# A hybrid mLSTM, GLA and sparse-attention block: one weight place more, one load in flight fewer, one large tile fewer, and a planner that counts changes of matmul kind

## The chip, the cores and the metric

The kernel runs on one core of a Trainium2 chip. A core has TensorE (PE, matrix multiply, with weight loads listed apart as PEld), VectorE (DVE), ScalarE (ACT), GpSimd (POOL) and SyncE (SP, which here only issues transfers), each with its own instruction stream; they meet at semaphores. The metric is device time of one execution in microseconds (us).

## The reference, cut to what matters

```python
def hybrid_layer(x, ...):                       # x: 1 x 512 x 1024, f32
    p = split_columns(rmsnorm(x, norm_g) @ w_in)
...
    hm = mlstm_chunkwise(q, k, v, li, lf)       # 4 heads of 256, behind a causal convolution and silu
    y_ml = rmsnorm(hm * sigmoid(ml_o)) * silu(ml_z)
    hg = gla_chunked(gla_q, gla_k, gla_v, la)   # 4 heads, chunks of 64
    y_gla = rmsnorm(hg) * silu(gla_r)
    hd = dsa_sparse_attention(dq, dk, dsa_v, iq, idx_k, iw, rel_bias, topk=128)
    y_dsa = hd * silu(dsa_z)
    return x + concatenate([y_ml, y_gla, y_dsa]) @ w_out

def reference(x, ...):
    for layer in range(2):
        x = hybrid_layer(x, ...)
    return x
```

## The kernel before, in words

Most of PE's work is the two projections of each layer. They are done to about f32 precision with one-pass f32r matmuls: weights and activations are split into a high and a low part, and three matmuls (`mm3`: high x high, low x high, high x low) make one product. The names: `xs` is the normed block of x before its transpose, `psx` the transpose, `xhi` and `xlo` its two parts; `pn`, `pt` and `pw` are the outputs of projections in PSUM (128x512). Between them lie matmuls of another kind (transposes, f32 matmuls): `psx`, `psga` (the decayed products of GLA; its operands `dec` and `qz` are made by POOL, ACT and DVE), `psq` (transposes of `qn`, the normed queries and keys of the sparse attention), and others. `psS` are the one-pass products of `ml_q` and `ml_k`. `zz` and `so` are gates, `sw` the mLSTM decay weights, for which the mask `negm` is loaded; `bs` is the bias of the sparse attention, loaded from `skew` and masked by POOL with `sel`, the result of the top-k selection (pairs of MAX8 and MATCH_REPLACE on DVE); `rq` is the scale of `qn`.

Weights come in 178 pieces of 128x1024 f32 (512 KB). SP loads a piece into `raw`; ACT copies it to `hi` in f32r; DVE makes `lo` = `raw` - `hi`. All three come from one pool of `W_BUFS` places of that size. `make_room` issues loads as long as places are free and fewer than `RAWS` pieces are loading or unsplit; it runs after each `lo` and after each `give_back`, which frees the two places of a piece after its last matmul. A piece counts as loaded `LOAD` = 4.5 us after its issue. The pool `t4` has `N_T4` large tiles of 4 KB per partition for everything else that is large.

The order of all instructions is decided while the program is built. Each instruction is recorded through a `Meter`, which asks `cost` for a duration and books it on a `Clock` per engine, with the dependencies. Work beside the projections (softmax, selection, gates, GLA, mLSTM) is written as generators in a `Background`; each `tick` between groups of 6 projection matmuls first calls `prepare` (at most one `lo` and one `hi`) and then steps those tasks that are due by the clock of PE. So any change of a cost or a pool shifts where tasks are put between the projection matmuls, on every engine. On the chip each engine takes its instructions in this order and waits at semaphores.

All instructions are recorded at one line, L178, so the rows below are told apart by their tiles.

```python
    def prepare():
        if half_done:
            p = half_done.pop()
            lo = w_tile("lo", F32R)
            nc.vector.tensor_sub(lo, p.raw, p.hi.bitcast(F32))
...
            make_room()
        if to_split and to_split[0].loaded <= clock.at["pe"] and state["used"] + 2 <= W_BUFS:
            p = to_split.pop(0)
...
            p.hi = w_tile("hi", F32R)
            nc.scalar.activation(p.hi, p.raw, AF.Copy)
            half_done.append(p)
```

Of the kernel before, what the change touches and what calls it, by code (L numbers as in the profile page):

```python
# [159 lines left out]
def free_size(ap):  # L160
    return math.prod(ap.shape[1:])


class Meter:


    def __init__(self, engine, name, clock):
        self.engine, self.name, self.clock = engine, name, clock
# [12 lines left out]
    def cost(self, op, args, kw):  # L181
        out = args[0]
        if op == "dma_start":
            return None
        if self.name == "pe":
            if op == "transpose":
                return 0.109
            n, one_pass = free_size(out), kw["rhs"].dtype == F32R
            if one_pass:
                return max(n, 256) / 2210 + 0.002  # L190
            if out.shape[0] == 64:
                return max(n / 950, 0.08)
            return max(4 * n, 256) / 2400 + 0.004
        n = free_size(args[1]) if op == "max" else free_size(out)
        pointers = sum(hasattr(v, "ap") and free_size(v) == 1 for v in (*args[2:], *kw.values()))
        accum = kw.get("accum_out") is not None
        if self.name == "act":
            switch = self.clock.ln != (args[2] == AF.Ln)
            self.clock.ln = args[2] == AF.Ln
            return 0.155 + n / 1138 + 0.09 * pointers + 0.12 * accum + 1.3 * switch  # L200
        if self.name == "dve":
            return 0.15 + n / 945 + 0.06 * min(pointers, 1) + 0.02 * accum
        if kw.get("op") == OP.pow:
            return 0.45 + 0.15 * n
        return 0.1 + n / (510 if op == "tensor_tensor" else 600) + 0.1 * (op == "tensor_tensor")


class Clock:
# [4 lines left out]
    def __init__(self):  # L213
        self.at = dict(pe=0.0, act=0.0, dve=0.0, pool=0.0, sync=0.0)
        self.now = 0.0
        self.ln = True
        self.written, self.touched = {}, {}
        self.rings = {}

    def begin(self):  # L220
        self.now = self.at["pe"]
# [29 lines left out]
    def book(self, engine, cost, outs, ins):  # L251
        at = self.at
        start = max([at[engine]] + [self.latest(self.written, engine, v) for v in ins]
                    + [self.latest(self.touched, engine, v) for v in outs])
        if cost is None:
            at[engine] = start + self.ISSUE
            end, engine = start + self.DMA, "dma"
        else:
            at[engine] = end = start + cost
        self.now = max(self.now, end)  # L260
        for v in outs:
            self.written.setdefault(v.name, {})[self.box(v)] = end, engine
        for v in outs + ins:
            self.touched.setdefault(v.name, {})[self.box(v)] = end, engine
# [69 lines left out]
def hybrid_kernel(ctx, tc, a, out, dbg=None):  # L334
# [12 lines left out]
            nc.gpsimd.dma_start(dbg[name], ap)  # L347

    ctx.enter_context(tc.manual_schedule())
    N_T4, N_T2 = 11, 19  # L350
    W_BUFS, RAWS, LOAD = 11, 3, 4.5
    const = ctx.enter_context(tc.tile_pool(name="const", bufs=1))
    par = ctx.enter_context(tc.tile_pool(name="par", bufs=2))
    wp = ctx.enter_context(tc.tile_pool(name="wp", bufs=2))
# [997 lines left out]
```

## Time and profile before

| what | value |
|---|---|
| runs, median of 3 | 1228.73 us (1228.69 to 1230.84) |
| profiled execution | 1227.63 us |
| its span, first to last instruction | 1225.9 us |
| mean granted clock of PE | 0.996 |
| busy: PE, PEld | 1198.3 us (98%), 970.6 us (79%) |
| busy: DVE, ACT, POOL | 835.1 us (68%), 600.6 us (49%), 171.0 us (14%) |
| transfers | 107.70 MB, 88 GB/s on the mean |

The profiled execution is 1.1 us faster than the median; 1.7 us of it lie outside the span. Busy shares are means over stages: PE's 98% says that it nearly always has a matmul under way, not that each runs at its fastest. In a timeline row, the numbers are the start, the duration of the row (of all instructions that it groups), the engine, the operation with its output and inputs, and in brackets the idle time ahead of it and what released it.

### The profile page before, as it was taken

How to read it: one execution, taken by the hardware profiler on the slowest of the kernel's cores; microseconds unless marked ns; L12 is line 12 of the kernel's file. 1: busy time of each engine (PE TensorE's matmuls, PEld its weight loads, DVE VectorE, ACT ScalarE, POOL GpSimd, SP SyncE). 2: the span in 40 equal slices, each digit the busy share in tenths (PEclk: the TensorE clock that was granted, in tenths of full speed). 3: DMA queues.
4: the chain of work that ended last, by engine and by line, in shares of the span. 5: the costliest groups of instructions: out<-in, count | busy, mean ns of one | idle time of the engine just before them, and what ended most of it. 6: DMA issues, size and time to landing. Idle time of an engine off the chain costs nothing. (4 is left out here: it accounts for less than half of the span.)

```text
span 1225.9 us, 16513 instructions
## 1 busy us (share of the span) xinstructions
PE 1198.3 (98%) x6004; PEld 970.6 (79%) x6004; DVE 835.1 (68%) x1650; ACT 600.6 (49%) x1334; POOL 171.0 (14%) x309
## 2 busy tenths in 40 slices
PE   6999899999999999999999999999999999999998
PEld 4877687888888887788879777888788888778887
DVE  5477797876777765355555888879867867544644
ACT  6565446554344354652366654474443443555421
POOL 2001221321000010210010023031210000122000
PEclk8999999999999999999999999999999999999999
DMA  5333122212332234132124222222222223233221
GB/s 195 108 98 104 44 92 72 86 61 55 105 108 69 70 119 129 53 112 86 69 70 128 63 86 79 80 73 86 71 70 86 79 85 104 70 112 112 69 82 73
DMA packets 35152, 107.70 MB, mean 88 GB/s; under 512 B 5028, under 2 KB 8388, under 8 KB 35072
## 3 DMA queue, kind: packets, MB, share of 16 engines
q1 hardware_dynamic: 33136, 104.89, 26.5%
q0 software_dynamic: 1200, 1.36, 0.3%
q8 instruction: 47, 0.77, 0.3%
q10 hardware_dynamic: 736, 0.41, 0.1%
q14 instruction: 33, 0.27, 0.1%
HBM read 104.48 MB, written 3.43 MB: 88 GB/s over the span
## 5 line engine op out<-in xcount | busy, mean ns | idle before, releaser
L178 DVE TENSOR_TENSOR lo<-raw,hi 128x1024 fp32r<-128x1024 f32 x178 | 219.1, 1231 | 140.2 <-ACT hi L178 133.5
L178 PE MATMUL pn<-hi,xhi 128*128 128x512 f32 x768 | 313.4, 408 | 0.4 <-ACT xhi L178 0.4
L178 PE MATMUL pn<-lo,xhi 128*128 128x512 f32 x768 | 305.2, 397 | 4.1 <-DVE lo L178 4.1
L178 PE MATMUL pn<-hi,xlo 128*128 128x512 f32 x768 | 304.1, 396 | 0.0
L178 ACT ACTIVATE hi<-raw 128x1024 fp32r<-128x1024 f32 x178 | 188.7, 1060 | 197.9 <-PE pn L178 96.8
L178 PEld LDWEIGHTS pn<-lo,xhi 128*128 128x128 f32 x768 | 145.1, 189 | 37.7 <-DVE lo L178 7.0
L178 PEld LDWEIGHTS pn<-hi,xlo 128*128 128x128 f32 x768 | 144.6, 188 | 35.8 <-DVE xlo L178 1.3
L178 PEld LDWEIGHTS pn<-hi,xhi 128*128 128x128 f32 x768 | 145.1, 189 | 33.2 <-issue 0.8
L178 PE MATMUL pt<-xhi,hi 128*128 128x512 f32 (+1 forms) x400 | 159.1, 398 | 0.0
L178 PE MATMUL pt<-xhi,lo 128*128 128x512 f32 (+1 forms) x400 | 154.6, 387 | 0.0
L178 PE MATMUL pt<-xlo,hi 128*128 128x512 f32 (+1 forms) x400 | 154.5, 386 | 0.0
L178 PE MATMUL pw<-hi,yhi 128*128 128x512 f32 x256 | 102.1, 399 | 0.8 <-DVE zz L178 0.8
L178 PE MATMUL pw<-hi,ylo 128*128 128x512 f32 x256 | 100.0, 391 | 0.0
L178 PE MATMUL pw<-lo,yhi 128*128 128x512 f32 x256 | 99.8, 390 | 0.0
L178 PEld LDWEIGHTS pt<-xhi,hi 128*128 128x128 f32 x400 | 75.2, 188 | 18.0 <-issue 3.9
L178 PEld LDWEIGHTS pt<-xhi,lo 128*128 128x128 f32 x400 | 75.3, 188 | 15.3
L178 PEld LDWEIGHTS pt<-xlo,hi 128*128 128x128 f32 x400 | 75.5, 189 | 12.7
L178 DVE TENSOR_TENSOR xr<-pw,xr 128x512 f32<-128x512 f32 x64 | 44.2, 690 | 58.7 <-PE pw L178 58.7
L178 DVE SCALAR_TENSOR_TENSOR cacc<-cbuf,pv,cacc 128x512 f32<-128x512 f32 x96 | 73.3, 763 | 2.5 <-ACT el L178 0.2
L178 PEld LDWEIGHTS pw<-hi,yhi 128*128 128x128 f32 x256 | 48.1, 188 | 10.5 <-DVE zz L178 1.2
L178 PEld LDWEIGHTS pw<-hi,ylo 128*128 128x128 f32 x256 | 48.0, 188 | 10.3
L178 PEld LDWEIGHTS pw<-lo,yhi 128*128 128x128 f32 x256 | 48.2, 188 | 9.3
(187 smaller groups left out, 1671.0 us busy)
## 6 DMA issues: line engine op xcount, KB each, us to landing
raw<-w_pack SPq DMA_DIRECT2D x178, 512.0 KB, 3.5
xr<-x SPq DMA_DIRECT2D x4, 512.0 KB, 7.3
negm<-negm SPq DMA_DIRECT2D x8, 256.0 KB, 3.7
bs<-skew SPq DMA_DIRECT2D x8, 256.0 KB, 4.0
out_dram<-xr SPq DMA_DIRECT2D x8, 256.0 KB, 2.0
bs<-skew SPq DMA_DIRECT2D x8, 192.0 KB, 4.5
skew<-flat POOLq DMA_DIRECT2D x1, 1280.0 KB, 16.1
bs<-skew SPq DMA_DIRECT2D x8, 128.0 KB, 4.5
```

Of the source, the lines that this page charges most:

```text
L178: return f(*args, **kw)
```

## The change

The weight pool gets 12 places (11 before), at most 2 pieces load or wait to be split (3 before), and the large tiles are 10 (11 before). In the planner, a transpose or a matmul that isn't one-pass is booked 0.085 us longer when the matmul ahead of it was a one-pass one.

```diff
@@ Meter.cost
             if op == "transpose":
-                return 0.109
+                switch = self.clock.leave()
+                self.clock.projecting = False
+                return 0.109 + switch
             n, one_pass = free_size(out), kw["rhs"].dtype == F32R
+            switch = 0.0 if one_pass else self.clock.leave()
+            self.clock.projecting = one_pass
             if one_pass:
                 return max(n, 256) / 2210 + 0.002
             if out.shape[0] == 64:
-                return max(n / 950, 0.08)
-            return max(4 * n, 256) / 2400 + 0.004
+                return max(n / 950, 0.08) + switch
+            return max(4 * n, 256) / 2400 + 0.004 + switch
@@ Clock
         self.ln = True
+        self.projecting = False
...
+    def leave(self):
+        return 0.085 * self.projecting
@@ hybrid_kernel
-    N_T4, N_T2 = 11, 19
-    W_BUFS, RAWS, LOAD = 11, 3, 4.5
+    N_T4, N_T2 = 10, 19
+    W_BUFS, RAWS, LOAD = 12, 2, 4.5
```

Every engine keeps the same set of instructions; their order changes in many places. Three of them follow.

The first is on PE, in the first layer, where the heads' scores `psS` begin beside the second pair of GLA products. `psga<-qz_100` and `psga<-qz_101` are GLA products of one level each, `x8` one burst (the trace lists it as 16). Before, the rows are these:

```order
L178 MATMUL pn<-hi,xlo 128x512
L178 MATMUL psga<-qz_100,dec 64x2x32 x8
L178 MATMUL psS<-ml_q,ml_k 128x512 x6
L178 MATMUL pn<-hi,xhi 128x512
L178 MATMUL pn<-lo,xhi 128x512
L178 MATMUL pn<-hi,xlo 128x512
L178 MATMUL pn<-hi,xhi 128x512
L178 MATMUL pn<-lo,xhi 128x512
L178 MATMUL pn<-hi,xlo 128x512
L178 MATMUL psS<-ml_q,ml_k 128x384 x6
```

And in the change these, where the row above the first is the 24th projection matmul since the `psga<-qz_101` burst (the 18th before):

```order
L178 MATMUL psS<-ml_q,ml_k 128x512 x6
L178 MATMUL pn<-hi,xhi 128x512
L178 MATMUL pn<-lo,xhi 128x512
L178 MATMUL pn<-hi,xlo 128x512
L178 MATMUL pn<-hi,xhi 128x512
L178 MATMUL pn<-lo,xhi 128x512
L178 MATMUL pn<-hi,xlo 128x512
L178 MATMUL psS<-ml_q,ml_k 128x384 x6
L178 MATMUL psga<-qz_100,dec 64x2x32 x8
```

The `psga` burst has moved behind two groups of `psS`, and the first `psS` behind six projection matmuls more. At the same place DVE has the selection's next pair put ahead of `ml_k` (a piece of the difference, `+` is the change):

```order
 L178 SCALAR_TENSOR_TENSOR cacc<-cbuf,cacc 128x512
 L178 COPY_PREDICATED att<-lev,psga 64x8x32 x2
+L178 MAX m_1272<-acc_642 128x8
+L178 MATCH_REPLACE acc_642<-m_1272,acc_642 128x512
 L178 TENSOR_TENSOR ml_k<-cacc,ml_k 128x512
 L178 TENSOR_TENSOR dec<-dec,gk 128x16x16
 L178 TENSOR_TENSOR qz_100<-dec,gq 64x256 x2
 L178 TENSOR_TENSOR val<-pn,vah 128x256
```

`ml_k` and the `qz` behind it come after two more instructions.

The second place is on SP, where the first layer's `bs` loads are issued (the piece of the difference; the second layer's reads the same but for the split of the last `raw` loads):

```order
 L178 DMA negm<-negm 128x512
-L178 DMA raw<-w_pack 128x1024 x20
+L178 DMA raw<-w_pack 128x1024 x19
 L178 DMA bs<-skew 128x512 x2
 L178 DMA bs<-skew 128x384 x2
 L178 DMA bs<-skew 128x128 x2
+L178 DMA raw<-w_pack 128x1024
 L178 DMA bs<-skew 128x256 x2
 L178 DMA raw<-w_pack 128x1024 x4
```

One `raw` load that stood ahead of the `bs` loads now stands behind six of them.

The third is on DVE, in the second layer, where gates `zz` free a PSUM bank that the next `pw` takes. Before:

```order
L178 SCALAR_TENSOR_TENSOR ylo<-psy,pv,yhi 128x128 x4
L178 TENSOR_TENSOR lo<-raw,hi 128x1024 x2
L178 SCALAR_TENSOR_TENSOR zz<-th,pn 128x512
L178 SCALAR_TENSOR_TENSOR so<-so,rm,zz 128x256 x2
L178 SCALAR_TENSOR_TENSOR zz<-th,pn 128x512
L178 SCALAR_TENSOR_TENSOR so<-so,rm,zz 128x256 x2
L178 TENSOR_TENSOR xr<-pw,xr 128x512 x2
```

In the change:

```order
L178 MATCH_REPLACE acc_5979<-m_8165,acc_5979 128x512
L178 TENSOR_TENSOR lo<-raw,hi 128x1024 x2
L178 SCALAR_TENSOR_TENSOR zz<-th,pn 128x512
L178 SCALAR_TENSOR_TENSOR so<-so,rm,zz 128x256 x2
L178 SCALAR_TENSOR_TENSOR zz<-th,pn 128x512
L178 SCALAR_TENSOR_TENSOR so<-so,rm,zz 128x256 x2
L178 TENSOR_TENSOR xr<-pw,xr 128x512
L178 TENSOR_TENSOR lo<-raw,hi 128x1024
```

Before, the last `lo` was issued in the same gap between PE's groups as the `zz`; now two groups of six projection matmuls lie between them, and the next `lo` stands behind both `zz`.

## Rows read from the trace of the kernel before

**Rows 1.** PE's waits by what released it; us in total, times, longest us
```profile
PE psq L178 <- ACT qn L178: 4.1, 2, 2.2
PE pn L178 <- DVE lo L178: 4.1, 6, 1.9
PE psga L178 <- DVE qz L178: 2.7, 1, 2.7
PE pw L178 <- DVE zz L178: 0.8, 1, 0.8
...
PE pn L178 <- ACT xhi L178: 0.4, 1, 0.4
```

**Rows 2.** Engines' busy us by stretch, PEclk; its heading and one row
```profile
core 0: us, PE busy (x) PEld busy (x) DVE busy (x) ACT busy (x) POOL busy (x), PEclk, DMA share, GB/s
...
130.00:150.00 20.00, 15.45 (x85) 12.03 (x85) 15.21 (x23) 5.48 (x12) 5.27 (x10) 0.91 0.12 41
```

**Rows 3.** Timeline, PE, 130 to 149 us
```profile
131.91 0.50 PE L178 MATMUL pn<-lo,xhi 128*128 128x512 f32 x1 [1.85 <-DVE lo L178]
...
137.47 0.69 PE L178 MATMUL psga<-qz,dec 128*64 128x64 f32 x16
...
145.24 1.12 PE L178 MATMUL psga<-qz,dec 128*64 128x64 f32 x16 [2.70 <-DVE qz L178]
...
146.29 2.73 PE L178 MATMUL psS<-ml_q,ml_k 128*128 128x512 f32 x6
...
148.86 0.40 PE L178 MATMUL pn<-hi,xhi 128*128 128x512 f32 x1
```

**Rows 4.** Timeline, PE, a burst between projection matmuls, 161 to 164 us
```profile
161.68 0.40 PE L178 MATMUL pn<-hi,xlo 128*128 128x512 f32 x1
162.01 0.69 PE L178 MATMUL psga<-qz,dec 128*64 128x64 f32 x16
162.63 0.50 PE L178 MATMUL pt<-xhi,hi 128*128 128x512 f32 x1
162.96 0.40 PE L178 MATMUL pt<-xlo,hi 128*128 128x512 f32 x1
163.20 0.40 PE L178 MATMUL pt<-xhi,lo 128*128 128x512 f32 x1
```

**Rows 5.** Timeline, ACT, 130 to 140 us
```profile
137.32 0.72 ACT L178 ACTIVATE sw<-negm,gn 128x512 f32<-128x512 f32 x1 [6.87 <-DMA negm<-negm]
```

**Rows 6.** Timeline, DVE, 130 to 143 us
```profile
130.64 2.53 DVE L178 TENSOR_TENSOR lo<-raw,hi 128x1024 fp32r<-128x1024 f32 x2
...
136.27 0.84 DVE L178 TENSOR_TENSOR qz<-dec,gq 64x256 f32<-64x256 f32 x2
...
142.25 0.69 DVE L178 TENSOR_TENSOR ml_k<-cacc,ml_k 128x512 fp32r<-128x512 f32 x1
```

**Rows 7.** Timeline, DVE, a pair of the top-k selection
```profile
108.32 0.69 DVE L178 MAX8 m<-acc 128x8 f32<-128x512 f32 x1
...
109.12 0.68 DVE L178 MATCH_REPLACE8 acc<-m,acc 128x512 f32<-128x512 f32 x1
```

**Rows 8.** Timeline, DVE, at 482 us
```profile
482.30 1.23 DVE L178 TENSOR_TENSOR lo<-raw,hi 128x1024 fp32r<-128x1024 f32 x1 [1.14 <-ACT hi L178]
```

**Rows 9.** Timeline, SP's queue, at 484 us
```profile
483.97 1.33 SPq L178 DMA_DIRECT2D bs<-skew  x3
```

**Rows 10.** Timeline, ACT, 480 to 494 us
```profile
480.66 0.66 ACT L178 ACTIVATE dsa_v<-pn 128x256 f32<-128x256 f32 x2 [0.74 <-PE pn L178]
...
493.97 1.28 ACT L178 ACTIVATE qn<-qn,rq 128x128 f32<-128x128 f32 x4 [5.94 <-POOL rq L178]
```

**Rows 11.** Timeline, POOL, at 488 us
```profile
487.75 4.81 POOL L178 TENSOR_TENSOR bs<-bs,sel 128x512 f32<-128x512 f32 x6 [27.77 <-DMA bs<-skew]
```

**Rows 12.** Timeline, PE, at 494 us
```profile
494.42 1.21 PE L178 MATMUL psq<-ident,qn 128*128 128x128 f32 x4 [1.96 <-ACT qn L178]
```

**Rows 13.** DMA issues (page, 6): KB each, median us to landing
```profile
raw<-w_pack SPq DMA_DIRECT2D x178, 512.0 KB, 3.5
```

**Rows 14.** ACT's waits, the row of the `raw` loads
```profile
ACT hi L178 <- DMA raw<-w_pack: 3.4, 1, 3.4
```

## The prediction

> **What bounds the kernel now.** I read the views from the coarse to the fine: busy shares, PE's waits, then the timelines of the places where PE waits. PE has work nearly always (the table of the profile), so only three things can move the end: PE's waits, its clock, and what PE pays when it goes from one kind of matmul to another. The waits [rows 1] are few: `psq` for ACT's `qn` (4.1 us, 2 times), `pn` for DVE's `lo` (4.1 us, 6 times), `psga` for DVE's `qz` (2.7 us, once), `pw` for DVE's `zz` (0.8 us), `pn` for `xhi` (0.4 us). Together 12.1 us. The two waits of the start, for the first data, are left out: no piece of the change is ahead of them. [...] The kinds: the step from a one-pass projection matmul into a `psga` burst is 0.33 us, and the second step behind it is 0.33 again [rows 4], 0.10 too much on either side.
>
> **What the change moves.** Every engine keeps its instructions; 5588 matmuls and transposes on PE, 1556 on DVE before and after. So no busy time is won or lost; only order and places change.
>
> *The clock term (0.085 for a change of kind).* Counted in the two orders, PE goes from one-pass matmuls to other kinds 133 times before and 126 times after. Seven fewer at 0.10 (one side of the step) to 0.19 (both) is -0.7 to -1.3 us; I take -0.7, since the transposes, most of the changes, are short and not shown by these rows.
>
> *12 places and two loading.* A piece holds one place while it loads, two once it is split. With one place more and one load fewer, two more places hold split weights. What that does to `lo` I counted in the orders: PE work at the cadence of [rows 4] between the place where `lo` is issued and its first matmul. Median 7.5 us before, 12.6 after; 24 pieces (without the first four) had under 2.9 us before, 4 after. DVE is behind PE by more than 2.9 us where PE waits for `lo`, so the five waits other than the one at 131.91 should go: 4.1 - 1.9 = 2.2 us [rows 1], and 0.1 each more, because the first matmul after an idle takes 0.50 and not 0.40 [rows 3, 4]: -2.7. Below: -2.2; above: nothing, if DVE falls back as much.
>
> *131 to 149 us.* Here the waits have one root: ACT stood 6.87 us for the `negm` transfer [rows 5], and DVE's `lo`, `qz` and `ml_k` [rows 6] ran one behind the other. The change leaves this root. The `lo` that PE awaited at 131.91 becomes that of the unit's fourth piece instead of its third, and is wanted six matmuls (1.4 us) later: the wait falls from 1.85 to 0.45. But PE is then at `psga` at 137.47 - 1.40 = 136.07 [rows 3], and `qz` ends at 136.27 + 0.84 = 137.11 [rows 6], so PE waits there, and only 0.3 us of the 1.4 is kept. Next, as front rows of the order show, 24 projection matmuls follow instead of 18, and then `psS` before the second `psga`. PE comes to `psS` at 137.15 + 0.62 (a burst of 16, [rows 4]) + 24 x 0.24 + 0.1 = 143.6. DVE has MAX8 and MATCH_REPLACE (108.32 to 109.12 + 0.68 = 109.80 in one case, 1.48 us [rows 7]) put ahead of `ml_k`: 142.25 + 1.48 + 0.69 = 144.4 [rows 6]. So a new wait of 0.8 us stands there. `psS` starts at 144.4 instead of 146.29 (-1.9), six projection matmuls more are behind PE (-1.4), the burst is still owed (+0.6): -2.7. At full clock the six `psS` take 1.5 instead of 2.57: -1.1. The second `qz` comes 2.3 us after `ml_k` (145.24 - 142.94), at 146.7, and the burst is now asked for at about 148.5: no wait. Sum -3.8. Bounds: -4.6 if `ml_k` is not late, -1.2 if the clock stays low and DVE is late by another MAX8 pair.
> [...]
>
> *psq, both layers.* SP issues in order. The `bs<-skew` loads went out at 483.97, right after the last `lo` (482.30 + 1.23 = 483.53) released the `raw` load that stood ahead of them [rows 8, 9]. POOL began on `bs` at 487.75, then made `rq`, ACT's `qn` ran at 493.97, and `psq` started at 494.42 after 1.96 us of idle [rows 10 to 12]. In the new order that last `raw` stands behind these loads, and the one now ahead waits for PE to have finished a unit, over by 480.66 at the latest (when ACT read it, [rows 10]). With 0.44 us for the issue (483.97 - 483.53), `bs` leaves at 481.1, 2.9 us earlier, and POOL and `qn` with it: 1.96 + 0.1 goes, and 0.9 us is to spare. The second layer has the same rows. -4.1 - 0.2 = -4.3; below nothing, if POOL is held by something else.
>
> *zz.* The `pw` that waited 0.8 us [rows 1] needs a bank that `zz` reads; DVE had a `lo` just before that `zz`. In the new order the last `lo` ahead of it is two groups of six matmuls earlier and the next stands behind both `zz` (front rows of the order): -0.9. Below: nothing, if that `lo` runs late.
>
> *Start.* `xhi` of the second block needs one `xs` ahead of it on ACT, not three, so 0.4 goes [rows 1]. ACT gets one `hi` (1.06 us) there early, in time in which it waits for a small load: nothing, or +1.1 if that load is earlier.
>
> *10 large tiles.* The shortest stretch of PE work between the last use of a large tile and the write that takes its place is 15.5 us before and 11.6 after, more than the longest stand of ACT here (6.87, [rows 5]). Nothing.
>
> **Sum.** -0.7 - 2.7 - 3.8 - 4.3 - 0.9 - 0.4 = -12.8. The profiled execution took 1227.63 us, 1.1 below the median of the runs (1228.73): 1214.8 by the profile, 1215.9 against the median. I say 1216. With every bound at its best it is 12.1 of waits, 0.8 for first matmuls, 1.1 of clock, 1.3 of kinds: -15.3.
>
> **The rivals.**
> *The waits move.* DVE's work is the same, and each early `lo` (1.23 us [rows 8]) stands ahead of something else. If half of the eight places that I clear get a wait of one `lo` back, 4 x 1.3 = 5.2 us returns: 1221. If all do, 10.4 returns: 1226. For it: `ml_k` above is a case of it. Against: DVE's `lo` before were late by order, not for want of time, since most of [rows 1] are single events.
> *No change.* The `bs` loads are held by another thing, and DVE's stage at 131 us keeps its 6 us: only 0.7 + 2.7 + 0.9 remain, and a wait or two return: 1226 to 1229. Against: [rows 9] shows SP issuing `bs` in one go once `raw` is out.
> *Slower: the loads are late.* With two loading, the PE work between a `raw` load's place and its `hi` on ACT falls from a median of 19.2 us to 11.0, and 52 pieces have under 6 us (8 before, without the first four). A load lands 3.5 us after its issue [rows 13], and it is issued only when a `lo` is done. ACT is in order, so a late `hi` holds `qn`, `relu`, `pT` behind it. It decides from 12.8 / 52 = 0.25 us of PE idle per such piece; at 0.5 us the time is 1215.9 + 26 = 1242. Against: the eight such pieces before cost nothing; ACT waited for a `raw` load once, at the start [rows 14].
> *Too few large tiles.* A large tile's writer then waits for its reader, PE behind it. This needs a reader that is 11.6 us late; one such wait per layer at the price of the `psga` wait (2.7) is +5.4: 1221.3. [...]
>
> **How the numbers follow.** Forecast 0.62 (1211 to 1219); waits move 0.17 (1219 to 1226); too few tiles 0.03; no change 0.10; slower by late loads 0.08. A measurement of this kernel can tell about 0.2%, 2.5 us. Faster by more than that is 0.62 + 0.17 + 0.03 = 0.82, within it 0.10, slower 0.08. The range, 1211 to 1226.5, leaves out the last two; the forecast's own is 1211 to 1219.
>
> **What would show it.** In PE's waits, `psq` for `qn` gone in both layers, with `bs` issued 3 us earlier; `pn` for `lo` once, under 1 us; `psga` for `qz` at 1.1 us, `psS` for `ml_k` at 0.8 us; the clock near 1.0 between 130 and 150 us. Wrong would be: ACT's `hi` waiting for `raw` many times, new waits of PE for ACT, or `psq` still waiting.

## The result, and the profile after

| what | before | after |
|---|---|---|
| median of the runs | 1229.47 us (4 runs, 1228.69 to 1230.84) | 1213.62 us (4 runs, 1211.41 to 1214.00) |
| profiled execution, its span | 1227.63 us, 1225.9 us | 1213.7 us, 1211.7 us |
| mean granted clock | 0.996 | 0.999 |

The ratio of the times is 0.9866, with an interval from 0.9849 to 0.9883: 1.3% faster. The forecast was 1216, from 1211 to 1226.5. Executions of one kernel differ with the granted clock: of 13 of the kernel before that were timed beside later runs, the seven with a mean of 0.993 or 0.994 took 1228.96 to 1229.93 us, the six with 0.995 to 0.997 took 1225.01 to 1228.17.

PE's waits after (us in total, times, longest us). The row of `psx` is the start; `psq`, `pw` and `xhi` of [rows 1] are gone, `psga` and `lo` are one short wait each, and that of `psst` stood there before too (0.6 us), though [rows 1] leaves it out:

```profile
PE psx L178 <- ACT xs L178: 12.0, 2, 8.3
PE psga L178 <- DVE qz L178: 1.1, 1, 1.1
PE psst L178 <- ACT kdn L178: 0.7, 1, 0.7
PE pn L178 <- DVE lo L178: 0.5, 1, 0.5
```

The stage of [rows 2] in the engines' busy times, with PEclk:

```profile
130.00:150.00 20.00, 18.40 (x109) 14.49 (x108) 17.30 (x30) 8.15 (x16) 4.94 (x11) 1.00 0.19 62
```

PE is busy 18.40 us of the 20 and not 15.45, and the granted clock is 1.00 on the mean and not 0.91. The same stretch in the timeline, first PE (beside [rows 3]), then the `ml_k` of DVE (beside [rows 6]):

```profile
131.29 0.50 PE L178 MATMUL pn<-lo,xhi 128*128 128x512 f32 x1 [0.49 <-DVE lo L178]
...
136.63 0.69 PE L178 MATMUL psga<-qz,dec 128*64 128x64 f32 x16 [1.12 <-DVE qz L178]
...
142.95 1.55 PE L178 MATMUL psS<-ml_q,ml_k 128*128 128x512 f32 x6
...
142.86 0.68 DVE L178 TENSOR_TENSOR ml_k<-cacc,ml_k 128x512 fp32r<-128x512 f32 x1
```

The wait for `lo` is 0.49 us (forecast 0.45), that for `qz` 1.12 (forecast 1.1), the six `psS` take 1.55 and not 2.73. But `psS` starts without a wait at 142.95, 0.09 us after DVE began the `ml_k` for which the forecast had it wait 0.8: what this `ml_k` makes can only be read by a later one of the six.

The timeline of SP, POOL, ACT and PE around the first `psq`, beside [rows 9 to 12]:

```profile
474.39 2.75 SPq L178 DMA_DIRECT2D bs<-skew  x6
477.24 0.38 SPq L178 DMA_DIRECT2D raw<-w_pack  x1
...
478.53 4.81 POOL L178 TENSOR_TENSOR bs<-bs,sel 128x512 f32<-128x512 f32 x6 [24.52 <-DMA bs<-skew]
...
484.75 1.28 ACT L178 ACTIVATE qn<-qn,rq 128x128 f32<-128x128 f32 x4 [3.18 <-POOL rq L178]
...
485.85 0.60 PE L178 MATMUL psq<-ident,qn 128*128 128x128 f32 x4
```

All six `bs` leave in one go, ahead of the `raw` load, and `psq` has no wait. By the matmuls done, PE is 6.45 us earlier at this place than in the kernel before, the gains ahead of it taken together; so beside PE's work `bs` left 483.97 - 474.39 - 6.45 = 3.1 us earlier than in the kernel before; the forecast said 2.9.

The sign of the slower rival is there too. ACT's waits for `raw` (beside [rows 14]):

```profile
ACT hi L178 <- DMA raw<-w_pack: 25.2, 19, 3.4
```

19 times instead of once, 25 us together; yet PE waits for no `hi` and nothing behind one, except at the start (below).

### The profile page after: what moved, and what is told of

The parts are those of the page before. It is cut to its first block, busy times and chain, and to the rows that moved or that the text cites. A ratio compares the mean times of both kernels' runs of the same rounds, so it can differ in the third digit from the quotient of the medians.

```text
span 1211.7 us, 16494 instructions
## 1 busy us (share of the span) xinstructions
PE 1193.6 (99%) x6004; PEld 970.3 (80%) x6004; DVE 832.8 (69%) x1650; ACT 600.3 (50%) x1334; POOL 168.3 (14%) x309
## 4 chain that ended last, share of the span: by engine, by line
PE 88%; DVE 1%; issue 0%; ACT 0%; ACTq 0%
PE pn L178 42%; PE pt L178 17%; PE pw L178 14%; PE psS L178 2%; PE pom L178 2%; PE psga L178 1%; PE pod L178 1%; PE psl L178 1%; PE pog L178 1%; PE psy L178 1%; PE pst L178 1%; PE pss L178 1%; PE psq L178 1%; PE psx L178 0%; PE psst L178 0%; DVE lo L178 0%
```

## The experiments

**What was in dispute.** The forecast took the sum as made by several moves in the order, each with its own cause. While comparing the traces I found rows of the kernel before that I had not used, of SP's queue (the second is for a comparison below) and of DVE's waits:

```profile
SPq L178 <- DVE lo L178: 651.6, 107, 21.1
...
SPq L178 <- PE pn L178: 90.0, 11, 24.5
...
DVE lo L178 <- PE pt L178: 4.8, 1, 4.8
```

So 107 times SP stood for a `lo` before it could issue its next transfer, and DVE once stood 4.78 us for PE to give back a place, and from there its timeline shows no gap until the `lo` of [rows 6]:

```profile
107.18 1.23 DVE L178 TENSOR_TENSOR lo<-raw,hi 128x1024 fp32r<-128x1024 f32 x1 [4.78 <-PE pt L178]
```

That made a second theory, of the *spare place*. A split piece holds two places and a loading one holds one. Eleven places with three loading are filled exactly by four split pieces (4 x 2 + 3); twelve with two loading by five (5 x 2 + 2). In a full pool a `raw` load has no place until the latest `lo` has freed one, and whatever is behind it on SP's queue, `negm` and `bs` among it, is late. Both the kernel before and the changed one are full; the variants below with one place more or one load fewer leave one spare.

**One part alone.** The pools without the clock term, then the term without the pools:

```diff
@@ pools_only (from the kernel before)
-    N_T4, N_T2 = 11, 19
-    W_BUFS, RAWS, LOAD = 11, 3, 4.5
+    N_T4, N_T2 = 10, 19
+    W_BUFS, RAWS, LOAD = 12, 2, 4.5
@@ clock_only (from the changed kernel)
-    N_T4, N_T2 = 10, 19
-    W_BUFS, RAWS, LOAD = 12, 2, 4.5
+    N_T4, N_T2 = 11, 19
+    W_BUFS, RAWS, LOAD = 11, 3, 4.5
```

> The pools of the change (12 places, 2 loading, 10 large tiles) without the planner's term for a change of kind. Theory: the two halves of the change act at different places. The pools bring lo earlier and take the raw load away from ahead of bs, so the waits of psq for qn, of pn for lo (but for the one at 131 us) and of pw for zz are gone; but the order of psS and the second psga at 145 us is that of the kernel before (psga first, 18 projection matmuls after the first psga, no MAX8 pair ahead of ml_k), so the psga wait of about 2.7 us and the half clock behind it are back: 1213.6 + 4.4 = 1218 us, clock about 0.91 to 0.95 between 130 and 150 us. Rival (the pools are the whole of it, the term only a fine detail): 1213.6 us, no psga wait above 1.2 us.

> The planner's term alone, with 11 places, 3 loading and 11 large tiles. Theory: psS stands ahead of the second psga, as in the change, so the psga wait and its half clock go (-3.9 us), 3 changes of kind fewer (-0.3 us); PE's waits for lo (6, 4.1 us) and psq's two waits for qn (4.1 us) stay, since the bs loads still stand behind a raw load that waits for lo: 1225 us. Rival (the term does nothing by itself): 1228 to 1230 us.

Measured: the pools alone 1221.93 us, ratio 0.9944 (0.9928 to 0.9961); the term alone 1227.87 us, 0.9993 (0.9982 to 1.0004). Together they give 15.9 us, apart 7.0 and 1.1, the last within the noise. Both times are above their theories' (1218 and 1225 us), and the traces are of the fastest execution of each (1219.73 and 1225.51 us). PE's waits in the first:

```profile
PE psga L178 <- DVE qz L178: 6.4, 4, 3.0
PE psst L178 <- ACT kdn L178: 0.7, 1, 0.7
PE pn L178 <- DVE lo L178: 0.5, 1, 0.5
```

Two of the four for `qz`, in its timeline:

```profile
143.52 0.69 PE L178 MATMUL psga<-qz,dec 128*64 128x64 f32 x16 [2.98 <-DVE qz L178]
...
263.48 0.69 PE L178 MATMUL psga<-qz,dec 128*64 128x64 f32 x16 [1.97 <-DVE qz L178]
```

PE's waits in the second:

```profile
PE psq L178 <- ACT qn L178: 5.7, 3, 2.9
PE pn L178 <- DVE lo L178: 3.8, 5, 1.8
```

The pools take away the waits for `lo`, `qn` and `zz`, as forecast; the term moves `psS` ahead of the second `psga` and takes away the wait for `qz`. Without the term the `psga` waits stay, and there is one more at 263 us. Each part opens waits that the other closes.

**Other sizes.** From the changed kernel, three loading, or eleven places, or thirteen (for which two small tiles go), so that one place is spare:

```diff
@@ raws3
-    W_BUFS, RAWS, LOAD = 12, 2, 4.5
+    W_BUFS, RAWS, LOAD = 12, 3, 4.5
@@ places11
-    W_BUFS, RAWS, LOAD = 12, 2, 4.5
+    W_BUFS, RAWS, LOAD = 11, 2, 4.5
@@ places13
-    N_T4, N_T2 = 10, 19
-    W_BUFS, RAWS, LOAD = 12, 2, 4.5
+    N_T4, N_T2 = 10, 17
+    W_BUFS, RAWS, LOAD = 13, 2, 4.5
```

> The changed kernel with 3 loading instead of 2 (12 places, 10 large tiles, the term). In its order lo is as late as before (median 7.5 us of PE work ahead of its first matmul, 24 pieces under 2.9 us), but the raw load ahead of bs waits for PE's release of an earlier piece and not for the last lo. Theory: psq's waits are gone, the stage at 145 us is as in the change, the waits for lo stay (about 3 us, with zz): 1213.6 + 3.5 = 1217 to 1221 us. Rival 1 (one place more is what helps, the number of loads does not matter): 1213 to 1214 us, no waits for lo. Rival 2 (psq was not held by SP's order): psq waits 2 us twice, 1225 us.

> The changed kernel with 11 places instead of 12 (2 loading, 10 large tiles, the term). In its order lo has a median of 7.0 us ahead of its first matmul (26 pieces under 2.9 us) and a raw load has 11.0 us to its hi (58 pieces under 6 us). Theory: waits for lo as in the kernel before or more (about 3 us), psq's waits gone, since the raw load ahead of bs waits for PE: 1217 to 1222 us. Rival (fewer loads in flight is what helps): 1213 to 1214 us. Rival (loads late): over 1228 us, with ACT's hi waiting for raw and PE behind it.

> The changed kernel with 13 weight places and two loading, for which two small tiles (2 KB) are given up (N_T2 17 instead of 19), so the planner's order differs too. One place is spare: the raw load ahead of negm and bs in most cases waits for an older piece's release and not for the last lo, and lo keeps its 12.6 us median. Theory: both sources of gain in one kernel, no psga wait and no psq wait, lo under 0.6 us: 1211 to 1212.5 us, 1 to 2 us under the change. Rival (two small tiles fewer hold tasks back): waits of new kinds and over 1214 us.

Measured: 1212.92 (ratio 0.9869, 0.9855 to 0.9884), 1211.74 (0.9863, 0.9849 to 0.9878) and 1212.84 (0.9872, 0.9856 to 0.9889). The first two should have been slower than the changed kernel and were not. Their `lo` is no farther ahead of its use than in the kernel before (median 7.5 and 7.0 us of PE work, against 12.6 in the changed kernel), so the distance that the forecast counted is not what the gain needs. What the three share is the spare place. The third, which has both the distance and the spare place, was forecast 1 to 2 us under the changed kernel and can't be told from it. The waits of SP and of DVE in the first, with no 4.8 us stand:

```profile
SPq L178 <- DVE lo L178: 107.0, 35, 7.5
DVE lo L178 <- PE pn L178: 0.9, 1, 0.9
```

**The prediction's root, `negm`.** The `negm` loads from POOL's queue, in the kernel before and in the changed one, and `bs` as well:

```diff
@@ before_negm_pool, before_both_pool, after_negm_pool
-            nc.sync.dma_start(nm, L["negm"][h:h + 1, :].to_broadcast([128, S]))
+            nc.gpsimd.dma_start(nm, L["negm"][h:h + 1, :].to_broadcast([128, S]))
@@ before_both_pool
-                nc.sync.dma_start(bs[hh], bias_rows(2 * g + hh, n))
+                nc.gpsimd.dma_start(bs[hh], bias_rows(2 * g + hh, n))
```

> The kernel before with the negm loads issued from POOL's queue instead of SP's; the orders of PE and DVE are the same, ACT's differs in a few places. Theory (a load on SP stands behind a raw load that waits for the last lo, since there is no spare place): negm comes when POOL reaches it, ACT's 6.9 us stand before sw near 131 us goes, so do the half clock at 145 us and most of the psga wait (2.7 us to about 0.9, since DVE still has the work); the wait for lo at 131.9 us and psq's two waits stay: 3 us less, about 1226 us. Rival (DVE alone sets that stage): psga still waits 2.7 us, no change.

> The same with the bs loads on POOL's queue too (PE's order differs in a few places late in each layer). Theory: psq's waits for qn (4.1 us) go as well, with nothing changed in the weights' places, the number of loads or the planner's costs: 7 us less than before, about 1222 us. What would be left of the change's gain is lo (3 us), zz, the first wait at 131 us. Rival (psq waits because qn or POOL is late by itself): psq waits 2 us twice, 1226 to 1229 us.

> The changed kernel with the negm loads on POOL's queue; the orders of PE, DVE and ACT are the same. Theory: ACT no longer stands 6.8 us near 130 us, but the psga wait there (1.1 us) is for a qz that DVE reaches only after 6.5 us of work without a gap, so PE gains at most 0.3 us: 1213 to 1214 us. Rival (the wait comes from negm as well): the 1.1 us goes, 1212.3 us.

Measured: 1229.88 (1.0014, 1.0005 to 1.0024), 1225.39 (0.9974, 0.9958 to 0.9990), 1214.69 (0.9890, 0.9875 to 0.9905). None came out at its theory's time (1226, 1222, and 1213 to 1214 us). In the second `psq` no longer waits, but PE stood twice for DVE's `so` ahead of `psy` (3.0 us together) and 5.4 us for `lo` (4.1 before). In the third the wait of 1.1 us for `qz` went, and one of 2.2 us for ACT's `dec` came at the same burst, with a granted clock of 0.91 from 130 to 150 us. In the first the wait for `qz` is gone, but that for `lo` grew from 1.85 to 2.45: DVE was slower where POOL issued the transfer and, behind it, ran its `dec`. The timeline of DVE and POOL there:

```profile
126.07 2.16 DVE L178 TENSOR_TENSOR ml_q<-cacc,ml_q 128x512 fp32r<-128x512 f32 x1
...
125.83 0.59 POOL L178 DMA_DIRECT2D negm<-negm  x1 [0.38 <-issue]
126.44 1.23 POOL L178 TENSOR_TENSOR dec<-ta 128x256 f32<-128x256 f32 x2
```

In the kernel before, this `ml_q` and the `cacc` ahead of it and behind it took 1.10 + 1.13 + 2.31 = 4.54 us; here 0.69 + 2.16 + 2.31 = 5.16. These 0.62 us match the 0.60 by which the wait for `lo` grew. Moving the transfer to POOL's queue brings a cost of its own, so the test was made again with ACT's queue:

```diff
@@ before_negm_act
-            nc.sync.dma_start(nm, L["negm"][h:h + 1, :].to_broadcast([128, S]))
+            nc.scalar.dma_start(nm, L["negm"][h:h + 1, :].to_broadcast([128, S]))
```

> The kernel before, with the negm loads issued from ACT's queue in place of SP's; nothing else. The prediction's root, that ACT's stand of 6.87 us for negm makes PE wait at 131.91 and at 145.24: ACT's wait for negm falls under 3 us, the psga wait of 2.7 us goes and the lo wait of 1.85 us falls under 0.5, 1223 to 1225 us. Rival, that DVE is late from its own stand of 4.8 us for a place near 107 us: that stand stays, PE still waits 1.5 us or more for lo near 132 us, 1226 to 1229 us.

Measured: 1225.78 us, ratio 0.9977 (0.9967 to 0.9987). The wait for `negm` and that for `qz` are gone, and DVE's stand and PE's wait for `lo` are where they were, in the timeline:

```profile
108.25 1.22 DVE L178 TENSOR_TENSOR lo<-raw,hi 128x1024 fp32r<-128x1024 f32 x1 [4.78 <-PE pt L178]
...
132.97 0.50 PE L178 MATMUL pn<-lo,xhi 128*128 128x512 f32 x1 [1.84 <-DVE lo L178]
```

The time lies between the theory's range and the rival's. The mean clock of the stage is again 0.91, in the engines' busy times:

```profile
130.00:150.00 20.00, 18.16 (x98) 14.03 (x98) 15.22 (x26) 8.07 (x16) 5.03 (x10) 0.91 0.11 41
```

But it is not the same loss. PE's timeline behind the wait for `lo`, first in the kernel before, then here, and here the `psS`:

```profile
132.71 0.40 PE L178 MATMUL pn<-lo,xhi 128*128 128x512 f32 x1
132.95 0.39 PE L178 MATMUL pn<-hi,xlo 128*128 128x512 f32 x1
...
134.51 0.63 PE L178 MATMUL pn<-hi,xhi 128*128 128x512 f32 x1
134.94 0.63 PE L178 MATMUL pn<-lo,xhi 128*128 128x512 f32 x1
...
145.72 1.66 PE L178 MATMUL psS<-ml_q,ml_k 128*128 128x512 f32 x6
```

In the kernel before, PE ran at full clock behind its 1.85 us for `lo` (a matmul every 0.24 us, 1.00 granted from 132 to 144 us) and at half behind the wait for `qz` (0.50 granted from 146 to 148 us). Here the six `psS` take 1.66 us, not 2.73, and the slow steps stand behind the wait for `lo` (a matmul every 0.43 us, to 137.3 us). A second such stretch lies at `psq`'s wait of 2.19 us at 1093.33, where the kernel before had none in its trace (1.00 granted from 1094 to 1100 us, behind 2.16 us); the mean clock of this execution is 0.994, against 0.996.

So the stage has two roots and not one: `negm` is that of the wait for `qz` and of the half clock behind it (3 us by the medians), and not that of the wait for `lo`, behind which the steps of 0.43 us stand in this run.

**The spare place, alone.** First one digit of the kernel before, with which the orders differ in places; then a place that the planner does not count, with which the order of PE, DVE, ACT, POOL and SP's loads is that of the kernel before, instruction by instruction:

```diff
@@ before_raws2
-    W_BUFS, RAWS, LOAD = 11, 3, 4.5
+    W_BUFS, RAWS, LOAD = 11, 2, 4.5
@@ before_spare
-    N_T4, N_T2 = 11, 19
+    N_T4, N_T2 = 10, 19
...
-        return wp.tile([128, 1024], dtype, tag="w", name=name, bufs=W_BUFS)
+        return wp.tile([128, 1024], dtype, tag="w", name=name, bufs=W_BUFS + 1)
```

> The kernel before with one number changed: two pieces loading in place of three, still 11 places, 11 large tiles and no clock term. Theory of the spare place: with 11 places, three loading ones and four split ones fill the pool exactly, so every raw load waits for the lo issued last, and DVE's lo stands 4.8 us for PE to give back a place near 107 us, which makes DVE late up to 145 us. With two loading, ten places are in use and one is spare: DVE's stand of 4.8 us near 107 us is gone, SP's queue waits for lo some 40 to 50 times and not 107, the psga and psq waits of PE are gone, the waits for lo may stay; 1215 to 1219 us. Rival, that the order of the planner's clock term is needed for the gain: the waits for psga and psq stay, 1226 to 1229 us.

> The kernel before with one place more in the weight pool that the planner does not know of: the pool has 12 places, the planner goes on counting 11 (and the large tiles are 10 to make room). Every engine's order of instructions is the same as before, so only waits for places can change. Theory of the spare place: SP's raw loads no longer wait for the lo just issued (107 times before, 30 to 50 here), negm and bs leave earlier, DVE's stand of 4.8 us near 107 us is gone, and with them PE's waits for qn (4.1 us), for qz (2.7 us) and for lo at 131.91 (1.85 us) and the low clock behind the latter; the waits for lo and zz that are late by order stay (2.2 and 0.8 us): 1215 to 1219 us. Rival, that the gain needs the other order (lo farther ahead of its use, psS ahead of psga): at most the 4.1 us of qn go, 1224 to 1229 us.

Measured: 1214.67 us, ratio 0.9882 (0.9867 to 0.9896), and 1216.87 us, ratio 0.9900 (0.9882 to 0.9919). In the second, the waits of PE and of SP:

```profile
PE psx L178 <- ACT xs L178: 11.5, 2, 8.3
PE pn L178 <- DVE lo L178: 1.9, 5, 0.7
PE pn L178 <- ACT xhi L178: 1.2, 1, 1.2
PE pw L178 <- DVE zz L178: 0.8, 1, 0.8
...
SPq L178 <- PE pn L178: 563.5, 80, 26.4
...
SPq L178 <- DVE lo L178: 99.6, 33, 7.4
```

In DVE's timeline the `lo` that stood 4.78 us:

```profile
102.58 1.22 DVE L178 TENSOR_TENSOR lo<-raw,hi 128x1024 fp32r<-128x1024 f32 x1
```

And the busy times of the stage:

```profile
130.00:150.00 20.00, 20.00 (x125) 15.99 (x125) 15.45 (x27) 8.99 (x18) 5.81 (x13) 1.00 0.20 67
```

The order is the old one, and the waits for `qn`, for `qz` and for `lo` at 131.91 are gone, with the low clock; those for `zz` and the small ones for `lo` stay, as the theory said. By [rows 1] and the clock term of the prediction that is 4.1 + 2.7 + 1.85 + 1.1 = 9.8 us; the span fell from 1225.9 to 1215.2, by 10.7, though the wait for `xhi` grew by 0.8. SP does not stand less: its waits for `lo` became waits for PE's release of an older piece (`PE pn` 80 times and not 11). What is gained is that a load, and what is queued behind it, leaves by an older release.

**A start without its small wait.** The version with eleven places and two loading, with the first `wa` load at the head of ACT's stream (the planner then moves eight `psx` of PE and one `xs` of ACT near the start):

```diff
@@ places11_wa
+    wa0 = t2("wa", 256)
+    nc.scalar.dma_start(wa0[64:80], a["gla_w_a"][0])
...
-        wa = t2("wa", 256)
-        nc.scalar.dma_start(wa[64:80], a["gla_w_a"][layer])
+        wa = t2("wa", 256) if layer else wa0
+        if layer:
+            nc.scalar.dma_start(wa[64:80], a["gla_w_a"][layer])
```

> The spare-place version (11 places, two loading, 10 large tiles, the clock term) with the first layer's small load of wa issued at the start of ACT's stream, not where it is first used. At the start ACT waits for this load and PE for ACT's xs (3.8 us longest). If that wait is bound by wa: 0.5 to 1.0 us less than the 1211.7 us of the version without it, 1210.7 to 1211.2 us. If it is bound by the first raw load or by x: 1211.7 us, no change.

Measured: 1214.36 us (1214.16 to 1214.55), ratio 0.9880 (0.9864 to 0.9897): not faster, and neither theory's number. The second `psx` comes earlier (18.94 us into the span, not 19.77), and the span is 1212.4 us, beside 1212.2 of the profiled execution without the edit. The traces show where the start's gain goes. At its hundredth matmul PE is 4.05 us ahead (32.61 us into the span, not 36.66; the granted clock of the first 30 us is 1.00, not 0.89). From there on the projections into `pw` give it back: the step between two of their matmuls has a median of 0.234 us here, and of 0.227 without the edit, over 738 steps 4.7 us. Why they are slower stays open.

**All of them.** Place arithmetic against what was measured. "SP for lo" is how often SP's queue stood for a `lo`; the runs of the kernel before beside them had medians from 1228.31 to 1229.47 us:

| places, loading, term | places in use when full | SP for lo | median us |
|---|---|---|---|
| 11, 3, no (before) | 11, none spare | 107 | 1229.47 |
| 11, 3, yes | 11, none spare | 104 | 1227.87 |
| 12, 2, no | 12, none spare | 109 | 1221.93 |
| 12, 2, yes (after) | 12, none spare | 98 | 1213.62 |
| 11 and one uncounted, 3, no | 11, one spare | 33 | 1216.87 |
| 11, 2, no | 10, one spare | 33 | 1214.67 |
| 12, 3, yes | 11, one spare | 35 | 1212.92 |
| 13, 2, yes | 12, one spare | 34 | 1212.84 |
| 11, 2, yes | 10, one spare | 35 | 1211.74 |

The best of them, 11 places with two loading and the term, is 0.15% below the changed kernel, with intervals of the ratios that overlap: no difference that can be told.

## Why the prediction was right, and where its reasons were not

The time, the sign and most terms were right. For each term I took the distance from one PE instruction to the next over its median for the same pair of forms, in both traces:

| term | forecast us | measured us |
|---|---|---|
| `lo` other than at 131.91 | -2.7 | -3.05 |
| 131 to 149 us | -3.8 | -4.1 |
| `psq`, both layers | -4.3 | -4.35 |
| `zz` | -0.9 | -0.9 |
| start | -0.4 | -0.6 |
| changes of kind, and what is left of the span | -0.7 | -1.2 |
| sum | -12.8 | -14.2 |

*The clock term.* Its remainder of -1.2 us is 0.17 for each of the seven changes of kind that went, between the 0.10 and the 0.19 of the forecast; the small waits in it are not told apart. But it isn't the planner's term that takes the seven away: counted in the orders, the pools alone have 126 changes of kind, as the changed kernel has, and the term alone has 130. The term is worth more by what it moves: alone nothing, on top of the pools 8.3 us.

*`lo`, `qn`, `zz`.* Went as worked out from the orders: three moves past one another on DVE and SP. The reason given for them, `lo` farther ahead of its use, is sufficient in the changed kernel (DVE's stand is still there, 4.79 us at 106.51, and SP still stands for `lo` 98 times, and PE hardly waits), but the runs with a spare place show that it isn't necessary.

*131 to 149 us.* Here a step failed: "Here the waits have one root: ACT stood 6.87 us for the `negm` transfer". With `negm` early the wait for `lo` was still 1.84 us; the wait for `qz` and the half clock behind it went. In the old order with a spare place DVE had no stand for a place near 107 us (one of 1.33 us for ACT's `relu` at 106.52), its `lo` pair began at 128.40 and not at 130.64, and PE did not wait for it. The spare place takes away both roots at once; that the stand alone makes the wait for `lo` is read from DVE's work without a gap between them, and no run took away the stand alone. The change left both roots and gained by order: `lo` one piece later in the unit, `psS` ahead of `psga`. The wait of 0.8 us for `ml_k` was the second miss, of the other sign: I had the first `psS` read what a later one of the six reads.

*The clock.* The -1.1 us is the six `psS` of [rows 3]: 148.86 - 146.29 = 2.57 us with a mean of 0.54 granted over them, against 1.5 at about the step of [rows 4], where 1.00 was granted. That the short waits of the change would leave the clock full was my estimate. In the change the six took 144.34 - 142.95 = 1.39 us, so -1.2: with waits of 0.49 and 1.12 us the granted clock was 1.00 over the stage. The runs don't order it by the longest single wait: the pools alone waited 2.98 us at 143.52 with 1.00 granted from 130 to 150, and 1.97 us at 263.48 with a mean of 0.91 from 255 to 275. Nor are equal waits followed by the same clock: behind 1.85 us at 131.91 it stayed full in the kernel before (1.00 from 132 to 144 us), behind 1.84 us for the same `lo` it fell with `negm` on ACT's queue (steps of 0.43 us, 0.91 on the mean from 130 to 150). So that the stage kept its clock in the change is measured, and what decides it stays open.

*The rivals.* "No change" needed `bs` held by another thing; it was held by the `raw` ahead of it: with that behind, `psq` had no wait. "The waits move" came true without the term, as two `psga` waits of 2.98 and 1.97 us. "The loads are late" showed its sign, 19 waits of ACT, and its price only at the start: ACT stood 1.11 us for `raw` and PE 3.77 us for the second `psx` (2.86 before), and the low clock there, 0.50 granted in both, was shorter (21.4 to 24.9 us, against 18.9 to 25.8). So the start's -0.6 near its forecast is luck: the forecast counted `xhi` alone, and a longer wait and a shorter low clock made up the rest. "Too few large tiles" fell: the uncounted place with the old order had ten too, and PE shows no wait there that the kernel before lacks.

*Room.* A place more took 12 us off without moving one instruction, and yet PE, busy for 98% of the span in the kernel before, shows no repeating gap in [rows 1]. What repeats stands on SP, and there the gaps stay: 107 waits for `lo` became 33, and 11 for `PE pn` became 80.

## What to carry to other kernels

Count the places of a rotating pool against what the planner lets be in use: a pool that is filled exactly makes most loads wait for the latest release (98 to 109 such waits here, against 33 to 35), and what is queued behind them is late, though PE shows only a few waits with different names. Look at what the transfer queue waits for, and not only how long, before explaining PE's waits one by one. To tell order from room, add a place that the planner does not count: the order stays, and only the waits for places can change.

## What the runs showed of the hardware

Moving a transfer to POOL's queue was not free for DVE: beside the issue (0.59 us on POOL) and POOL's next operation, `dec`, one DVE operation took 2.16 us, against 1.13 with a part of `dec` alone beside it and 0.69 with POOL idle, and the three around it took 0.62 us more together. What of this is the issue and what the shifted `dec` is not told apart; in the changed kernel the same edit made them only 0.19 us longer (4.77 and not 4.58), with 1.11 us for the operation beside the issue. With the same transfer on ACT's queue these DVE operations took 1.09, 1.13 and 2.31 us, as in the kernel before.
